# The assembly of a triangular inverse, moved from the scan's chain of steps into a background process

## The chip, the core and the metric

One core of a Trainium2 chip runs the whole kernel. The time is the device time of one execution in microseconds (us). The engines are PE (TensorE: matrix products, with its weight loads as PEld), DVE (VectorE), ACT (ScalarE), POOL (GpSimd) and SP (SyncE, which here only issues transfers). Each has its own queue of instructions and works through it in order; semaphores tie the queues together.

## The reference

One layer of a hybrid encoder on 2048 tokens of 1024 features, with 16 meta tokens ahead of them. One projection of `h` feeds two branches. Branch A is a gated DeltaNet with 8 heads: a short convolution, normed q and k, and a recurrence over chunks, in which a unit lower triangular system is solved for each chunk:

```python
lower = jnp.where(strict, jnp.einsum('bhnid,bhnjd->bhnij', k_beta, k) * decay, 0.0)
rhs = jnp.concatenate([v_beta, k_beta * jnp.exp(g_cum)[..., None]], axis=-1)
sol = lax.linalg.triangular_solve(lower + jnp.eye(CHUNK, dtype=f32), rhs, left_side=True, lower=True, unit_diagonal=True)
...
def step(S, inp):
    u_c, w_c, attn_c, q_c, k_c, gl_c = inp
    v_new = u_c - jnp.einsum('bhik,bhkv->bhiv', w_c, S)
    o_c = jnp.einsum('bhik,bhkv->bhiv', q_c, S) + jnp.einsum('bhij,bhjv->bhiv', attn_c, v_new)
    S = S * gl_c[..., None, None] + jnp.einsum('bhik,bhiv->bhkv', k_c, v_new)
    return S, o_c
```

Branch B is a sliding-window attention with sinks. Both branches are gated, projected, merged by gates computed from `h`, projected once more, added to `h` and layer-normed.

## The kernel before

**Tiles.** The 2048 tokens are worked in four blocks of 512 columns. A float32 operand is split into a high and a low part, and a projection of 128 output features over 512 tokens is 24 products of 128x128 by 128x512 (8 slices of the inner dimension, three products of parts each). These products, all on line L308, are the fill of the program: nearly all of PE's work.

**Order.** The program is one Python generator that writes instructions in the order in which every engine then takes them. `proj` yields behind every six products; this is one step, and one call of `tick()`. In `run(fill, streams, rates)` each step of the fill moves two streams by a fraction of a step: `chain`, which is `stage_c` of the groups 0 to 3 and then the attention `swa`, and `side`, which prepares the groups (`stage_b0`, `stage_b1`, `stage_b2`). Beside them run background processes, started with `bg(...)`: a process that yields a number n comes again n steps later, one that yields a condition comes when it holds. So the number of steps between two instructions sets how many of PE's products lie between them, and in every engine's queue what lies ahead of each.

**DeltaNet.** Two heads form a group, 128 tokens a chunk, four chunks a block. `conv_unit` writes the convolution of a projection: ACT copies the bank out, DVE adds three shifted products (L706, 128x512 each), ACT takes a tanh (L709), DVE multiplies (L711). `stage_b1(g)` transposes k (L779), forms the k·k products of the group in two banks, and DVE masks and scales them into `LT` (five small operations L796 to L800, then eight times L803), all eight 128x128 matrices of a group side by side. `stage_b2(g)` forms attn and transposes q (L876; ACT squares them, L878) and v.

`inverse(g)` is a background process that inverts the 32x32 diagonal blocks: a transfer to DRAM and back rearranges them, POOL solves them column by column (L829, L831), another transfer brings them back as `XT`, and after `DMA[5]` = 4 steps POOL copies XT into LT (L845).

`stage_c(g)` begins by putting the rest of the inverse together. DVE transposes XT into XN (L894, 128x256), ACT copies it into N64; PE forms `py` (L907, 16 small products), ACT copies it into Y (L912); PE forms `px` (L917 and L919, 24 products), ACT copies it into N64 and LT; then the same for 64x64 blocks with `py2`, Y2 and `px2`. Five plain yields of the chain lie between. Then comes the scan over the four chunks, in three parts a chunk: k·S (L958) into the bank `pks`, and R on DVE (L961); pw = LT·R (L966), q·S (L968), and wd from pw on DVE (L971) and ACT (L973); pu (L979) and the new S on DVE (L981). `out` is a background process that two steps later adds attn·wd (L947) in the same bank `pks` and DVE takes it up (L949).

**Banks.** Transposes, k·k, the scan and the assembly take their PSUM banks in turn from a pool of four, called `ps` in the trace; the projections have another four, `acc`. A bank is written again when the fourth request after it comes, and has to have been read by then.

**Other neighbours.** On DVE the low part of a split weight or of a branch output (L144, 128x1024) stands in the same queue, as do the small operations of the meta tokens in block 0 (`meta_heads`).

Of the kernel before, what the change touches and what calls it, by code (L numbers as in the profile page):

```python
# [73 lines left out]
def hybrid_kernel(  # L74
# [355 lines left out]
    def meta_heads(g, mstage, ok):  # L430

        h0 = 2 * g
        yield lambda: ok("kT", 1) and "es" in meta
        km, kt = yield from meta_conv(g, mstage, 0)
        pk = bank()
        for hh in range(2):
            T.matmul(pk[:NM, hh * NM:hh * NM + NM], km[:, hh, :], km[:, hh, :], start=True, stop=True)
# [155 lines left out]
    def block(b, nextx):  # L593
# [215 lines left out]
        def inverse(g):  # L809
# [36 lines left out]
            d["XT"] = XT  # L846

        def stage_b2(g):
# [4 lines left out]
            sq = tiny([P, 2, NC4], "sq")  # L853
# [32 lines left out]
        def stage_c(g):  # L886

            d, h0 = gr[g], 2 * g
            yield from until(lambda: "XT" in d and "vtok" in d)
            kT, qT, ktok, vtok, attn, LT = (d[n] for n in ("kT", "qT", "ktok", "vtok", "attn", "LT"))  # L890
            sq, cj, ce, XT = (d[n] for n in ("sq", "cj", "ce", "XT"))
            eg, neg = gates["eg"], gates["neg"]
            XN = tiny([P, 8, 32], "XN", 1)
# [1 line left out]
            N64 = tiny([64, 8, 64], "N64", 1)
            if first and g == 0:
                G.memset(N64[0:32, :, 32:64], 0.0)
                state["N64"] = N64
            N64 = state["N64"]
            A.activation(N64[0:32, :, 0:32], XN[0:32], AF.Copy)  # L900
            A.activation(N64[32:64, :, 32:64], XN[32:64], AF.Copy)
            yield

            py = bank()
            for m in range(8):
                for a, bq in ((0, 32), (64, 96)):
                    T.matmul(py[bq:bq + 32, m * 32:m * 32 + 32], LT[a:a + 32, m, bq:bq + 32], XN[a:a + 32, m, :],  # L907
                             start=True, stop=True, tile_position=(a, bq))
            Y = tiny([P, 8, 32], "Y", 1)
            for s in range(2):  # L910
                bq = 64 * s + 32
                A.activation(Y[bq:bq + 32], py[bq:bq + 32, 0:256].rearrange("p (m i) -> p m i", m=8), AF.Copy)  # L912
            yield
            px = bank()
            for m in range(8):
                for a, bq in ((0, 32), (64, 96)):
                    T.matmul(px[a:a + 32, m * 32:m * 32 + 32], Y[bq:bq + 32, m, :], XT[bq:bq + 32, m, :],  # L917
                             start=True, stop=True, tile_position=(bq, a))
                T.matmul(px[32:64, m * 32:m * 32 + 32], XT[32:64, m, :], Y[32:64, m, :], start=True, stop=True, tile_position=(32, 32))  # L919
            A.activation(N64[32:64, :, 0:32], px[32:64, 0:256].rearrange("p (m i) -> p m i", m=8), AF.Copy)  # L920
            for s in range(2):
                a, bq = 64 * s, 64 * s + 32
                A.activation(LT[a:a + 32, :, bq:bq + 32], px[a:a + 32, 0:256].rearrange("p (m i) -> p m i", m=8), AF.Copy)
            yield

            py2 = bank()
            for m in range(8):
                T.matmul(py2[64:128, m * 64:m * 64 + 64], LT[0:64, m, 64:128], N64[:, m, :], start=True, stop=True, tile_position=(0, 64))
            Y2 = s2([P, 8, 64])
            A.activation(Y2[64:128], py2[64:128, :].rearrange("p (m i) -> p m i", m=8), AF.Copy)  # L930
            yield
            px2 = bank()
            for m in range(8):
                T.matmul(px2[0:64, m * 64:m * 64 + 64], Y2[64:128, m, :], LT[64:128, m, 64:128], start=True, stop=True, tile_position=(64, 0))
            A.activation(LT[0:64, :, 64:128], px2[0:64, :].rearrange("p (m i) -> p m i", m=8), AF.Copy)
            yield
# [7 lines left out]
            def out(c, pks, wd):  # L944
                yield 2
                for hh in range(2):
                    T.matmul(pks[:, hh * P:hh * P + P], attn[:, hh, c, :], wd[:, 0, hh, :], start=True, stop=True)  # L947
                yield 2
                V.tensor_tensor(out=o[:, :, c, :], in0=pks[:, 0:256].rearrange("p (h d) -> p h d", h=2), in1=o[:, :, c, :], op=ALU.add)  # L949
                yield 1  # L950
                for hh in range(2):
                    A.activation(junk, o[:, hh, c, :], AF.Square, accum_out=so[:, hh, c:c + 1])
                d["so", c] = True

            for c in range(NC4):
# [558 lines left out]
```

## Time and profile before

| | |
|---|---|
| median of 3 runs (lowest, highest) | 2658.24 us (2656.61, 2660.33) |
| the profiled execution | 2659.29 us |
| its span, first to last instruction | 2657.5 us |
| PE busy, share of the span | 2606.1 us, 98% |
| DVE busy | 1573.0 us, 59% |
| ACT busy | 1223.3 us, 46% |
| POOL busy | 764.3 us, 29% |
| mean granted clock of PE, share of full | 0.992 |

Busy times are the sums of an engine's instructions; matrix products overlap and their ends are modelled. An engine can be idle as long as PE does not wait for it. The granted clock is given for any stretch; 1.00 is 2.4 GHz and 0.50 is 1.2 GHz. The four blocks end at about 721, 1361, 2002 and 2645 us.

### The profile page before, as it was taken

What the parts mean: (1) busy time and instruction counts of PE and PEld (TensorE: products, weight loads), DVE (VectorE), ACT (ScalarE), POOL (GpSimd) and SP (SyncE); (2) the same over time, 40 slices, a digit from 0 to 9 for tenths busy, and PEclk for the clock granted to TensorE, in tenths of its full rate; (3) what the DMA queues carried; (4) which work ended last, traced back from release to release, by engine and by line L of the source; (5) the groups of instructions that cost most, each with busy time, mean ns of one, the idle gap of its engine ahead of it and who ended that gap; (6) DMA issues with size and microseconds to landing.
All of it is one profiled execution on the core that took longest, in us unless ns stands there. A gap on an engine that the chain in (4) does not pass through costs nothing.

```text
span 2657.5 us, 44100 instructions
## 1 busy us (share of the span) xinstructions
PE 2606.1 (98%) x15308; PEld 2185.0 (82%) x15308; DVE 1573.0 (59%) x3959; ACT 1223.3 (46%) x3248; POOL 764.3 (29%) x1702
## 2 busy tenths in 40 slices
PE   9999999999999999999999999999999999999998
PEld 7777778888888888888887888888888788888886
DVE  6779858844464655762465564675347466476335
ACT  4556546542244544653324554565232455465422
POOL 2544324432055430110106433110102644111022
PEclk9999999999999999999999999999999999999999
DMA  7654556643574454664466445575347544466533
GB/s 256 202 177 166 190 185 186 203 159 102 192 251 148 144 173 143 206 196 149 150 213 194 136 148 168 168 212 180 122 158 237 176 143 149 153 202 207 167 101 136
DMA packets 243534, 461.63 MB, mean 174 GB/s; under 512 B 78024, under 2 KB 136160, under 8 KB 243312
## 3 DMA queue, kind: packets, MB, share of 16 engines
q1 hardware_dynamic: 243312, 458.82, 54.7%
q8 instruction: 121, 1.98, 0.3%
q14 instruction: 101, 0.83, 0.1%
HBM read 379.89 MB, written 78.82 MB: 173 GB/s over the span
## 4 chain that ended last, share of the span: by engine, by line
PE 61%; DVE 3%; POOL 2%; DMA 2%; ACT 1%; issue 1%; SPq 1%; DVEq 0%; POOLq 0%; ACTq 0%
PE acc L308 44%; PE ps L1127 2%; PE ps L1092 1%; POOL X L831 1%; POOL tm L829 1%; PE ps L968 1%; PE ps L958 1%; PE ps L966 1%; PE ps L979 1%; PE ps L947 1%; PE ps L1145 1%; DVE s L706 1%; PE acc L1395 1%; PE acc L1397 1%; PE acc L1398 1%; PE ps L858 1%
## 5 line engine op out<-in xcount | busy, mean ns | idle before, releaser
L308 PE MATMUL acc<-xh,wh 128*128 128x512 f32 x1800 | 740.3, 411 | 0.0
L308 PE MATMUL acc<-xl,wh 128*128 128x512 f32 x1800 | 711.2, 395 | 0.0
L308 PE MATMUL acc<-xh,wl 128*128 128x512 f32 x1800 | 476.3, 396 | 0.0
L308 PEld LDWEIGHTS acc<-xh,wh 128*128 128x128 f32 x1800 | 342.7, 190 | 60.7 <-issue 0.6
L308 PEld LDWEIGHTS acc<-xl,wh 128*128 128x128 f32 x1800 | 343.4, 191 | 58.7
L308 PEld LDWEIGHTS acc<-xh,wl 128*128 128x128 f32 x1800 | 331.2, 189 | 67.4 <-issue 0.5
L273 ACT ACTIVATE wh<-wr 128x1024 fp32r<-128x1024 f32 (+1 forms) x246 | 258.2, 1049 | 278.6 <-PE acc L308 158.8
L706 DVE SCALAR_TENSOR_TENSOR s<-st,cw,s 128x512 f32<-128x512 f32 x288 | 233.7, 812 | 70.3 <-ACT st L701 63.4
L144 DVE TENSOR_TENSOR wl<-wr,wh 128x1024 fp32r<-128x1024 f32 (+2 forms) x125 | 161.9, 1295 | 157.4 <-ACT wh L273 138.5
L308 PE MATMUL acc<-y,wh 128*128 128x512 f32 x1024 | 250.0, 392 | 0.0
L829 POOL TENSOR_TENSOR tm<-X,g 128x60 f32<-128x60 f32 (+24 forms) x496 | 169.8, 342 | 261.7 <-DMA g<-d 226.3
L308 PEld LDWEIGHTS acc<-y,wh 128*128 128x128 f32 x1024 | 189.1, 188 | 37.3
L308 PE MATMUL acc<-xh,wr 128*128 128x512 f32 x624 | 208.9, 402 | 0.0
L1244 POOL TENSOR_TENSOR g<-g 128x512 f32<-128x512 f32 x32 | 69.9, 2184 | 432.7 <-DVE g L1237 432.7
L831 POOL TENSOR_TENSOR X<-X,tm 128x60 f32<-128x60 f32 (+24 forms) x496 | 165.9, 335 | 38.9
L1237 DVE SCALAR_TENSOR_TENSOR g<-g,acc 128x512 f32<-128x512 f32 x64 | 44.0, 687 | 203.2 <-PE acc L308 203.0
L1073 POOL TENSOR_TENSOR g<-mo,slp 128x32 f32<-128x32 f32 x128 | 41.1, 331 | 389.3 <-DVE mn L1094 363.7
L1129 ACT ACTIVATE s<-ps 104x512 fp32r<-104x512 f32 (+2 forms) x128 | 76.5, 597 | 146.5 <-PE ps L1127 145.3
L308 PEld LDWEIGHTS acc<-xh,wr 128*128 128x128 f32 x624 | 116.2, 188 | 22.9
L1228 ACT ACTIVATE g<-acc,bg__162 128x512 f32<-128x512 f32 x64 | 44.2, 690 | 190.3 <-PE acc L308 189.7
L308 PE MATMUL acc<-y,wl 128*128 128x512 f32 x512 | 129.2, 390 | 0.0
L308 PE MATMUL acc<-xl,wr 128*128 128x512 f32 x312 | 122.2, 392 | 0.0
(329 smaller groups left out, 4668.4 us busy)
## 6 DMA issues: line engine op xcount, KB each, us to landing
wr<-in_wfm_dram SPq DMA_DIRECT2D x214, 512.0 KB
wl<-ws SPq DMA_DIRECT2D x165, 512.0 KB
wr<-ws SPq DMA_DIRECT2D x78, 512.0 KB
wh<-ws SPq DMA_DIRECT2D x75, 512.0 KB
ws<-wl SPq DMA_DIRECT2D x68, 512.0 KB
g<-kd SPq DMA_DIRECT2D x240, 96.0 KB
ws<-wh SPq DMA_DIRECT2D x38, 512.0 KB
wr<-in_wo_dram SPq DMA_DIRECT2D x32, 512.0 KB
```

What stands on the lines that cost most here:

```text
L144: eng.tensor_tensor(out=out_, in0=src, in1=f(hi), op=ALU.subtract)
L273: A.activation(hi[:, k], raw[:, k], AF.Copy)
L308: T.matmul(ps, w_[:, k, :], r_(k), start=(n == 0), stop=(n == 3 * NK - 1))
L706: V.scalar_tensor_tensor(out=acc, in0=st[:, 3 - d:TB + 3 - d], scalar=cw[:, s, 3 - d:4 - d], in1=acc, op0=ALU.mult, op1=ALU.add)
L829: G.tensor_tensor(out=tm[:, :n, :r], in0=X[:, :n, j:j + 1].to_broadcast([P, n, r]), in1=L[:, j:j + 1, j + 1:].to_broadcast([P, n, r]), op= ...
L831: G.tensor_tensor(out=X[:, :n, j + 1:], in0=X[:, :n, j + 1:], in1=tm[:, :n, :r], op=ALU.add)
L1073: G.tensor_tensor(out=sr[kv]["bias"][:, ch, :, 192:208], in0=mo[:, ch:ch + 1, :].to_broadcast([P, 2, NM]), in1=slp[:, 2 * kv:2 * kv + 2].u ...
L1127: T.transpose(out=pT[0:kt, j * 256 + rt * P:j * 256 + rt * P + P], in_=Pt[:, ch, rt, s + j * kt:s + j * kt + kt], identity=ident)
L1129: A.activation(ph[0:kt], pT[0:kt], AF.Copy)
L1228: A.activation(gt_[u][:, br, :], ps, AF.Tanh, scale=0.5, bias=bg_[:, 8 * br + u:8 * br + u + 1])
L1237: V.scalar_tensor_tensor(out=t[:, br, :], in0=t[:, br, :], scalar=1.0, in1=ps, op0=ALU.add, op1=ALU.mult)
L1244: G.tensor_tensor(out=m[:, u % 2, :], in0=t[:, 0, :], in1=t[:, 1, :], op=ALU.add)
```

## The change

The block from XN to `px2` leaves `stage_c` and becomes the end of `inverse(g)`, a background process. Its parts no longer lie one yield of the chain apart, but a number of steps, `JOIN`. The copy of XT into LT comes seven steps after its load instead of four. `stage_c` waits for `d["T"]`, the whole inverse, before it begins, and then starts with the scan. `out` requests a bank of its own instead of writing into `pks`. `cj`, `ce` and `sq` get three buffers. `meta_heads(g)`, which runs in block 0 alone, also waits until the meta tokens of group g - 1 are done, and its k·k products move down by one step. No instruction is added or removed on any engine.

```diff
-DMA = (1, 3, 4, 1, 2, 4)
+DMA = (1, 3, 4, 1, 2, 7)
+JOIN = (5, 4, 3, 3, 3)
...
     def meta_heads(g, mstage, ok):
-        yield lambda: ok("kT", 1) and "es" in meta
+        yield lambda: ok("kT", 1) and "es" in meta and (g == 0 or ("S", g - 1) in meta)
         km, kt = yield from meta_conv(g, mstage, 0)
-        pk = bank()
-        for hh in range(2):
-            T.matmul(pk[:NM, hh * NM:hh * NM + NM], km[:, hh, :], km[:, hh, :], start=True, stop=True)
...
+        pk = bank()
+        for hh in range(2):
+            T.matmul(pk[:NM, hh * NM:hh * NM + NM], km[:, hh, :], km[:, hh, :], start=True, stop=True)
+        yield 1
...
-            cj = tiny([P, 2, NC4], "cj")
+            cj = tiny([P, 2, NC4], "cj", 3)
...
         def inverse(g):
...
             yield DMA[5]
             for q in range(4):
                 G.tensor_copy(LT[32 * q:32 * q + 32, :, 32 * q:32 * q + 32], XT[32 * q:32 * q + 32])
-            d["XT"] = XT
+            d["XT"] = True
+            XN = tiny([P, 8, 32], "XN", 1)
+            V.transpose(out=XN.rearrange("p s i -> p (s i)"), in_=XT.rearrange("p s i -> p (s i)"))
...
+            A.activation(N64[0:32, :, 0:32], XN[0:32], AF.Copy)
+            A.activation(N64[32:64, :, 32:64], XN[32:64], AF.Copy)
+            yield JOIN[0]
+
+            py = bank()
...
+            yield JOIN[1]
+            px = bank()
...
+            yield JOIN[2]
+
+            py2 = bank()
...
+            yield JOIN[3]
+            px2 = bank()
...
+            yield JOIN[4]
+            d["T"] = True
...
         def stage_c(g):
-            yield from until(lambda: "XT" in d and "vtok" in d)
+            yield from until(lambda: "T" in d and "vtok" in d)
-            XN = tiny([P, 8, 32], "XN", 1)
...
-            d["T"] = True
-            def out(c, pks, wd):
+            def out(c, wd):
                 yield 2
+                pks = bank()
                 for hh in range(2):
                     T.matmul(pks[:, hh * P:hh * P + P], attn[:, hh, c, :], wd[:, 0, hh, :], start=True, stop=True)
...
-                bg(out(c, pks, wd))
+                bg(out(c, wd))
```

What this does to the queues shows in three places of DVE's, all in block 1; blocks 2 and 3 have the same. In the names, `XN` is the transposed XT, `sk`, `cj` and `ce` are the scales of a group, `g` are buffers of the large pool, `s` of the small one and `S` is the state of a group. The changed kernel's lines are shifted: L706 became L709, L711 became L714, L796 to L803 became L799 to L806, L894 became L851, L961 became L965, L971 became L975, L981 became L985, and L144 became L146.

The first place is the transpose XN of group 0. The kernel before, DVE:

```order
L711 SCALAR_TENSOR_TENSOR g_8931<-s_8909,s_8870 128x512
L894 STREAM_TRANSPOSE XN_8949<-XT_8874 128x256
L796 TENSOR_SCALAR sk_8728<-sk_8728 128x8
L797 RECIPROCAL cj_8912<-sk_8728 128x8
L798 TENSOR_TENSOR cj_8912<-cj_8912,gm4be_8122 128x8
L799 TENSOR_SCALAR ncj_8913<-cj_8912 128x8
L800 TENSOR_TENSOR ce_8914<-cj_8912,eg_8256 128x8
L803 SCALAR_TENSOR_TENSOR g_8911<-ps_8915,ncj_8913,g_8581 128x128 x4
L803 SCALAR_TENSOR_TENSOR g_8911<-ps_8916,ncj_8913,g_8581 128x128 x4
L706 SCALAR_TENSOR_TENSOR s_8941<-st_8939,cw,s_8941 128x512 x3
```

The changed kernel, DVE, the same place:

```order
L803 TENSOR_TENSOR ce_8930<-cj_8928,eg_8272 128x8
L806 SCALAR_TENSOR_TENSOR g_8927<-ps_8931,ncj_8929,g_8597 128x128 x4
L806 SCALAR_TENSOR_TENSOR g_8927<-ps_8932,ncj_8929,g_8597 128x128 x4
L709 SCALAR_TENSOR_TENSOR s_8957<-st_8955,cw,s_8957 128x512 x3
L851 STREAM_TRANSPOSE XN_9016<-XT_8890 128x256
L714 SCALAR_TENSOR_TENSOR g_8947<-s_8999,s_8957 128x512
```

The transpose has moved from ahead of the masks of group 1 to behind them and behind three convolution steps.

The second place is chunk 2 of the scan of group 0. The kernel before, DVE, from R of that chunk on:

```order
L961 SCALAR_TENSOR_TENSOR s_9566<-ps_9563,neg_8280,g_8673 128x128 x2
L971 TENSOR_SCALAR s_9586<-ps_9581,ce_8406 128x128 x2
L949 TENSOR_TENSOR g_8673<-ps_9464,g_8673 128x2x128
L706 SCALAR_TENSOR_TENSOR s_9577<-st_9575,cw,s_9577 128x512 x3
L981 SCALAR_TENSOR_TENSOR S_85<-S_85,eg_8256,ps_9632 128x128 x2
```

The changed kernel, DVE, from R of that chunk on:

```order
L965 SCALAR_TENSOR_TENSOR s_9634<-ps_9631,neg_8296,g_8689 128x128 x2
L799 TENSOR_SCALAR sk_9367<-sk_9367 128x8
L800 RECIPROCAL cj_9595<-sk_9367 128x8
L801 TENSOR_TENSOR cj_9595<-cj_9595,gm4be_8138 128x8
L802 TENSOR_SCALAR ncj_9596<-cj_9595 128x8
L803 TENSOR_TENSOR ce_9597<-cj_9595,eg_8272 128x8
L806 SCALAR_TENSOR_TENSOR g_9594<-ps_9598,ncj_9596,g_9141 128x128 x4
L806 SCALAR_TENSOR_TENSOR g_9594<-ps_9599,ncj_9596,g_9141 128x128 x4
L851 STREAM_TRANSPOSE XN_9665<-XT_9507 128x256
L709 SCALAR_TENSOR_TENSOR s_9624<-st_9622,cw,s_9624 128x512 x3
L975 TENSOR_SCALAR s_9683<-ps_9678,ce_8422 128x128 x2
```

Between R and wd of this chunk there now stand a group's scales and masks, a transpose and three convolution steps, where there was nothing; `ps_9678` (pw) is the bank that `ps_9598` was.

The third place is the scan of group 1 beside the second half of kT of group 3. The kernel before, DVE:

```order
L961 SCALAR_TENSOR_TENSOR s_10288<-ps_10285,neg_8280,g_9306 128x128 x2
L706 SCALAR_TENSOR_TENSOR s_10274<-st_10272,cw,s_10274 128x512 x3
L949 TENSOR_TENSOR g_9306<-ps_10171,g_9306 128x2x128
L971 TENSOR_SCALAR s_10334<-ps_10329,ce_8914 128x128 x2
L711 SCALAR_TENSOR_TENSOR g_10262<-s_10327,s_10274 128x512
```

The changed kernel, DVE, the same place:

```order
L985 SCALAR_TENSOR_TENSOR S_86<-S_86,eg_8272,ps_10240 128x128 x2
L709 SCALAR_TENSOR_TENSOR s_10231<-st_10229,cw,s_10231 128x512 x3
L965 SCALAR_TENSOR_TENSOR s_10288<-ps_10285,neg_8296,g_9277 128x128 x2
L146 TENSOR_TENSOR y_10297<-g_9317,y_10193 128x1024
L714 SCALAR_TENSOR_TENSOR g_10219<-s_10283,s_10231 128x512
```

The last operation of the convolution of kT now stands behind R and the low part of a branch output, where it stood behind wd.

## Rows read from the trace of the kernel before

**Rows 1.** Busy time by stretches: us, each engine, clock, DMA share, GB/s

```profile
721.00:1361.00 640.00, 637.38 (x3689) 539.21 (x3688) 356.96 (x892) 291.93 (x777) 165.70 (x412) 1.00 0.56 172
600.00:700.00 100.00, 100.00 (x443) 82.81 (x442) 38.49 (x37) 30.02 (x31) 17.51 (x8) 1.00 0.44 142
```

**Rows 2.** PE's waits, blocks 1 to 3: line, releaser: us, times, longest

```profile
PE ps L917 <- ACT Y L912: 6.7, 4, 3.7
PE ps L917 <- DMA d<-g: 2.3, 1, 2.3
PE ps L907 <- DVE sk L796: 1.2, 1, 1.2
```

**Rows 3.** Timelines, group 0's assembly: start, us, engine, operation [wait <- releaser]

```profile
811.66 0.45 DVE L894 STREAM_TRANSPOSE XN<-XT 128x256 f32<-128x256 f32 x1 [3.48 <-DMA XT<-d]
815.49 2.79 DVE L706 SCALAR_TENSOR_TENSOR s<-st,cw,s 128x512 f32<-128x512 f32 x3
818.31 0.63 ACT L709 ACTIVATE s<-s 128x512 f32<-128x512 f32 x1 [5.18 <-DVE s L706]
819.39 0.24 PE L917 MATMUL ps<-XT,Y 32*32 32x32 f32 x2 [2.25 <-DMA d<-g]
...
2095.29 0.45 DVE L894 STREAM_TRANSPOSE XN<-XT 128x256 f32<-128x256 f32 x1 [6.00 <-DMA XT<-d]
```

**Rows 4.** Busy time and clock in short stretches, columns as in rows 1

```profile
245.60:252.00 6.40, 3.67 (x23) 2.72 (x25) 5.71 (x27) 2.06 (x8) 5.22 (x18) 1.00 0.00 1
360.10:366.70 6.60, 6.05 (x18) 3.65 (x17) 5.11 (x16) 2.03 (x4) 2.37 (x1) 0.50 0.37 110
820.90:824.10 3.20, 3.20 (x9) 2.43 (x8) 2.25 (x3) 2.09 (x7) 0.00 (x0) 0.50 0.84 204
1459.20:1465.80 6.60, 6.12 (x59) 4.91 (x60) 2.92 (x4) 3.94 (x10) 1.91 (x8) 0.50 0.79 235
2096.00:2103.00 7.00, 3.51 (x44) 2.63 (x41) 6.11 (x16) 1.44 (x4) 6.35 (x9) 1.00 0.81 283
```

**Rows 5.** PE's timeline, parts of the scan and transposes of kT

```profile
867.86 0.61 PE L958 MATMUL ps<-S,g 128*128 128x128 f32 x4
869.69 0.60 PE L966 MATMUL ps<-s,g 128*128 128x128 f32 x4
...
934.41 0.60 PE L779 MATMUL ps<-cm,g 128*128 128x128 f32 x4
...
977.72 0.60 PE L966 MATMUL ps<-s,g 128*128 128x128 f32 x4
981.35 0.60 PE L979 MATMUL ps<-s,g 128*128 128x128 f32 x4
```

**Rows 6.** DVE's timeline at the same places, and a low part in block 0

```profile
174.56 1.21 DVE L144 TENSOR_TENSOR wl<-wr,wh 128x1024 fp32r<-128x1024 f32 x1
...
868.51 0.61 DVE L961 SCALAR_TENSOR_TENSOR s<-ps,neg,g 128x128 f32<-128x128 f32 x2 [0.24 <-PE ps L958]
...
876.76 0.13 DVE L796 TENSOR_SCALAR sk<-sk 128x8 f32<-128x8 f32 x1
877.68 2.16 DVE L803 SCALAR_TENSOR_TENSOR g<-ps,ncj,g 128x128 f32<-128x128 f32 x8
880.25 2.33 DVE L706 SCALAR_TENSOR_TENSOR s<-st,cw,s 128x512 f32<-128x512 f32 x3 [0.41 <-ACT st L701]
...
933.30 0.90 DVE L711 SCALAR_TENSOR_TENSOR g<-s,s 128x512 f32<-128x512 f32 x1
```

**Rows 7.** PE's waits in block 0, 104 to 721 us, columns as in rows 2

```profile
PE ps L779 <- DVE g L711: 5.5, 2, 3.0
PE ps L876 <- ACT g L878: 5.4, 2, 2.7
...
PE ps L979 <- DVE s L971: 1.7, 1, 1.7
PE ps L917 <- ACT Y L912: 1.3, 2, 1.2
```

More of the change, by code (lines that the diff above doesn't have):

```diff
@@ L845, in inverse @@
                 G.tensor_copy(LT[32 * q:32 * q + 32, :, 32 * q:32 * q + 32], XT[32 * q:32 * q + 32])
-            d["XT"] = XT
+            d["XT"] = True
+            XN = tiny([P, 8, 32], "XN", 1)
+            V.transpose(out=XN.rearrange("p s i -> p (s i)"), in_=XT.rearrange("p s i -> p (s i)"))
+            N64 = tiny([64, 8, 64], "N64", 1)
+            if first and g == 0:
+                G.memset(N64[0:32, :, 32:64], 0.0)
+                state["N64"] = N64
+            N64 = state["N64"]
@@ new lines, in inverse @@
+            A.activation(N64[0:32, :, 0:32], XN[0:32], AF.Copy)
+            A.activation(N64[32:64, :, 32:64], XN[32:64], AF.Copy)
+            yield JOIN[0]
+            py = bank()
+            for m in range(8):
+                for a, bq in ((0, 32), (64, 96)):
+                    T.matmul(py[bq:bq + 32, m * 32:m * 32 + 32], LT[a:a + 32, m, bq:bq + 32], XN[a:a + 32, m, :],
+                             start=True, stop=True, tile_position=(a, bq))
+            Y = tiny([P, 8, 32], "Y", 1)
@@ new lines, in inverse @@
+            for s in range(2):
+                bq = 64 * s + 32
+                A.activation(Y[bq:bq + 32], py[bq:bq + 32, 0:256].rearrange("p (m i) -> p m i", m=8), AF.Copy)
+            yield JOIN[1]
+            px = bank()
+            for m in range(8):
+                for a, bq in ((0, 32), (64, 96)):
+                    T.matmul(px[a:a + 32, m * 32:m * 32 + 32], Y[bq:bq + 32, m, :], XT[bq:bq + 32, m, :],
+                             start=True, stop=True, tile_position=(bq, a))
+                T.matmul(px[32:64, m * 32:m * 32 + 32], XT[32:64, m, :], Y[32:64, m, :], start=True, stop=True, tile_position=(32, 32))
@@ new lines, in inverse @@
+            A.activation(N64[32:64, :, 0:32], px[32:64, 0:256].rearrange("p (m i) -> p m i", m=8), AF.Copy)
+            for s in range(2):
+                a, bq = 64 * s, 64 * s + 32
+                A.activation(LT[a:a + 32, :, bq:bq + 32], px[a:a + 32, 0:256].rearrange("p (m i) -> p m i", m=8), AF.Copy)
+            yield JOIN[2]
+            py2 = bank()
+            for m in range(8):
+                T.matmul(py2[64:128, m * 64:m * 64 + 64], LT[0:64, m, 64:128], N64[:, m, :], start=True, stop=True, tile_position=(0, 64))
@@ new lines, in inverse @@
+            Y2 = s2([P, 8, 64])
+            A.activation(Y2[64:128], py2[64:128, :].rearrange("p (m i) -> p m i", m=8), AF.Copy)
+            yield JOIN[3]
+            px2 = bank()
+            for m in range(8):
+                T.matmul(px2[0:64, m * 64:m * 64 + 64], Y2[64:128, m, :], LT[64:128, m, 64:128], start=True, stop=True, tile_position=(64, 0))
+            A.activation(LT[0:64, :, 64:128], px2[0:64, :].rearrange("p (m i) -> p m i", m=8), AF.Copy)
+            yield JOIN[4]
+            d["T"] = True
@@ L852, in stage_b2 @@
             kT, qT, E, sk = d["kT"], d["qT"], d.pop("E"), d["sk"]
[L853 removed]
+            sq = tiny([P, 2, NC4], "sq", 3)
             attn = g4([P, 2, NC4, P])
@@ L888, in stage_c @@
             d, h0 = gr[g], 2 * g
-            yield from until(lambda: "XT" in d and "vtok" in d)
+            yield from until(lambda: "T" in d and "vtok" in d)
             kT, qT, ktok, vtok, attn, LT = (d[n] for n in ("kT", "qT", "ktok", "vtok", "attn", "LT"))
-            sq, cj, ce, XT = (d[n] for n in ("sq", "cj", "ce", "XT"))
+            sq, cj, ce = (d[n] for n in ("sq", "cj", "ce"))
             eg, neg = gates["eg"], gates["neg"]
-            XN = tiny([P, 8, 32], "XN", 1)
-            V.transpose(out=XN.rearrange("p s i -> p (s i)"), in_=XT.rearrange("p s i -> p (s i)"))
@@ L895, in stage_c @@
[L895 to L936, printed above, removed]
             if first:
                 yield from until(lambda: ("S", g) in meta)
-            d["T"] = True
```

2 lines of the change are left out of this document (1 added, 1 removed).

## The prediction

> **What bounds the kernel now.** I read the busy time by stretches first. In block 1 the TensorE (PE) is busy 637.38 of 640 us while VectorE (DVE), ScalarE (ACT) and GpSimd (POOL) are busy 357, 292 and 166 us [rows 1]. So only what makes PE stand still, or run at a lower clock, can move the end. Undisturbed, PE starts a product every 0.226 us (443 in 100 us) [rows 1]. Next come PE's waits by line. In blocks 1 to 3 nearly all of them belong to one place, the second pair of small products that assembles the inverse (`px`, L917): 6.7 us behind the ACT copy into Y (L912), 2.3 behind a DMA, and 1.2 at the first pair (L907), 10.2 us in all [rows 2]. Group 0 of each block is the one that waits.
>
> The engine rows tell how. DVE arrives at the transpose of XT (L894) at once and stands there 3.48 us, because the transfer of XT has not landed; behind it in DVE's queue lie the masks L803 and three convolution steps L706, which end at 818.28; ACT's tanh L709 waits 5.18 us for those, the Y copy stands behind that tanh, and PE reaches L917 and waits 2.25 us [rows 3]. After this wait, and after those of blocks 2 and 3 (up to 3.7 us [rows 2]), the granted clock is at 0.50, the lower of its two levels (1.2 GHz): for 3.2 us in block 1, 6.6 in block 2 and again 3.2 in block 3, for which block 1's row stands [rows 4]. At half speed half of such a stretch is lost: 6.5 us of 13.0.
>
> **What the change removes.** XN is now transposed behind its transfer by seven steps instead of four (a step is six products, 6 x 0.226 = 1.36 us), and `px` stands nine steps (12.2 us) behind XN, where it stood four (5.4 us). On DVE the masks and the L706 now lie ahead of the transpose (first order piece), so they no longer wait for the transfer. The longest of DVE's waits at L894 was 6.00 us, in block 3 [rows 3]; three more steps, 4.1 us, leave 1.9 of it, and 12.2 us lie between it and L917. I take all of 10.2 + 6.5 = **16.7 us** in blocks 1 to 3 as gone. It is a gain only as far as nothing else is late there, which is the next part.
>
> **What costs nothing by count.** Every instruction of the assembly stays (one transpose, nine ACT copies, 56 small matmuls per group); the loads of XT on SP's queue, POOL's four copies L845 and the ACT copies only move. POOL is busy a quarter of block 1, so three more steps in front of its copies are covered; if they were late, the next group's solve would be, which starts seven steps later. The scan of group 0 starts at step 81 instead of 69 (counting the yields), the attention at 185 instead of 174, and its last output is put down at step 272 instead of 261. The products that take it up come after step 283, where both streams are drained; in block 0 it is 286 against 287. So one step (1.36 us) of cover is left in block 0; without it PE would wait for the attention's output, at most a few us once. Third buffers for cj, ce and sq remove a wait that no row shows: nothing.
>
> **What it adds.** The scan runs 10 to 12 steps later against work that has not moved, and meets other neighbours. Three such places in each of blocks 1 to 3 can be priced.
>
> *A, pw of chunk 2 of group 0 (L966).* `out` now takes a bank of its own, so the four banks turn faster, and pw gets the bank of the first half of group 1's k·k products, which the first four L803 must have read. In the second order piece these stand behind R (L961). From PE's start on L958: DVE begins R at +0.65 (867.86 to 868.51), R 0.61, the five small operations 0.92 (876.76 to 877.68), half of 2.16 for four L803, 1.08: 3.26 us. PE gets to L966 1.83 us after L958 (867.86 to 869.69) [rows 5, 6]. Wait 1.4.
>
> *B, pu of the same chunk (L979).* PE: 1.83 + 1.43 + 3.63 (977.72 to 981.35) = 6.89. DVE: 3.26 + 1.08 + 0.45 for L894 + 2.33 for three L706 + about 0.6 for the two products of wd = 7.7 [rows 3, 5, 6]. Wait 0.8.
>
> *D, the second half of kT of group 3 (L779).* Before, DVE's last convolution step L711 ran 933.30 to 934.20 and PE began at 934.41, with nothing to spare [rows 5, 6]. In the third order piece R and a weight's low part (L144, 1.21 us) now stand before it: 0.65 + 0.61 + 1.21 + 0.90 = 3.4, less the 1.83 in which PE gets there from L958, as in A. Wait 1.5.
>
> None of these meetings occurs in the trace of before. Below, each is bounded by nothing (DVE ahead by a few tenths, as at 934.41); above by its wait plus 0.46 us, what three L706 took more at 815.49 than at 880.25 [rows 3, 6]. A gain is excluded: PE does not wait there now. I take the worked values, since each is a sum of rows: 3.7 us a block, **11.1 us** in three, bounds 0 and 15.
>
> *Block 0* carries the meta tokens as well, and nearly every meeting there becomes another. Waits that go: L917 1.3, the first of two at L779 5.5 - 3.0 = 2.5, L876 5.4, L979 1.7, together 10.9 [rows 7], and half of the 6.6 us at clock 0.50 after 360 us [rows 4], 3.3: 14.2. New places of the same kind, where PE in the new order stands one or two steps behind a DVE or ACT operation with a queue ahead of it: L966 twice, L779 twice, the meta tokens' products (now behind a gate), L876, and the transposes of group 0's output. Seven, at the mean of the four waits L779, L876 and L979, (2.5 + 5.4 + 1.7)/4 = 2.4: 16.8. Net **+2.6**, bounds -7 (only three of them real) and +8 (all at 2.7, the longest at L876, and as much time at the lower clock as before).
>
> **The sum.** -16.7 + 11.1 + 2.6 = -3.0. Against the profiled execution, 2659.29 us (span 2657.5), it is 2656.3. That execution lay 1 us over the median, 2658.24; the same difference gives **2655.2**, 0.11% faster. About 0.2% (5.3 us) is what a measurement of this kernel can tell from no change.
>
> **Rivals.** *R1: the new meetings are free.* If DVE runs ahead by one step at A, B and D, the 16.7 us stay gained and block 0 comes out even: 2641.5. For it: the same kind of meeting at 934.41 cost nothing, and DVE is idle 44% of block 1. Against it: at each of the three, DVE's rows add up to more than PE's.
>
> *R2, on the other side: the waits take the clock with them.* The place is A and D in blocks 1 to 3. The waits of 2.25 us and more at L917 were followed by the lower clock; the 1.2 at L907, which ended at 2095.9 us, was not, nor was one of 2.7 at L876 in block 0, which ended at 248.6 [rows 2, 4, 7]. It decides if A and D reach about 2.3: then 0.9 + 0.8 more idle and one stretch of 3.2 us, 1.6 lost, per block: 3 x 3.3 = 9.9, so 2665.
>
> The Trainium skill, "TensorE: Matmul & The Clock Gate", section "What's actually happening", has it that "the default state is throttled, and activity releases the throttle"; by that rule each new pause of PE is a chance to fall back, which is R2's time. The rows bear it out at L917 and not after the 1.2 and the 2.7; A, B and D were worked out shorter than the shortest wait with which it holds, so R2 is not the forecast.
>
> *R3: the change does not do what it says.* The wait at L917 stays, since the transfer of XT is late by more than the added steps, or another operation holds up the Y copy: 2658.2 + 11.1 + 2.6 = 2672. Against it: 12.2 us of products between XN and `px` against an ACT wait of 5.18 [rows 3].
>
> **How the numbers follow.** Forecast 0.48; its own range is 2649 to 2661 (faster 0.17, same 0.29, slower 0.02). R1 0.24 (0.22, 0.02, 0). R2 0.21 (0, 0.06, 0.15). R3 0.07 (0, 0.01, 0.06). Faster 0.39, same 0.38, slower 0.23. The range reaches from R1 to R2's end, 2641 to 2667, and leaves out R3 and the tails of block 0's bounds.
>
> **What would show it.** Right: no PE wait at `px` of group 0 and clock 1.00 there; PE waits of 1 to 2 us at pw of chunk 2 of group 0 behind the masks, at pu behind wd, and at kT's transposes behind the last convolution step, once each per block; block 0 with as much PE idle as before. R1: no PE wait of 0.5 us in blocks 1 to 3. R2: windows at clock 0.50 right after the new waits. R3: `px` still behind the Y copy. What would make it wrong: a meeting that I did not find in blocks 1 to 3, or block 0, where seven places were priced by a mean.

## The result and the profile after

The changed kernel takes 2675.75 us (median of six, 2675.22 to 2678.50), the kernel before 2658.0 beside it: 1.0067 times as long, interval 1.0054 to 1.0080. The forecast was 2655.2, the range 2641 to 2667. The page and the span:

```profile
PE 2614.0 (98%) x15308; PEld 2184.0 (82%) x15308; DVE 1575.9 (59%) x3959; ACT 1221.6 (46%) x3248; POOL 763.8 (29%) x1702
core 0: 2675.4 us, clock 0.991
```

PE's starts give the blocks' lengths, from the first product of one to that of the next: 734.0, 641.3, 641.3 and 642.9 us, where the kernel before has 716.9, 639.8, 641.4 and 643.3. So block 0 lost 17.1 us and the other three 1.0 together. PE's waits by line in blocks 1 to 3 (line, releaser, us in all, times, longest), against [rows 2]:

```profile
PE ps L970 <- DVE g L806: 3.9, 3, 1.3
PE ps L782 <- DVE g L714: 3.8, 3, 1.3
PE ps L1014 <- DVE s L1138: 1.1, 3, 0.4
PE ps L924 <- DVE g L714: 0.9, 3, 0.3
```

The waits at `px` (L917, now L874 and L876) have gone, and so has the lower clock in these blocks. In their place stand A (pw, L970) and D (kT, L782), once in each block, and four small ones, of which two are shown. In block 0 nearly every row is another than in [rows 7]. (L876 there is the transposes of v, not of q as said above, and L878 the scaled copy out of their bank; L876 is L924 here.)

```profile
PE ps L782 <- DVE g L714: 7.4, 2, 4.0
PE ps L512 <- DVE s L508: 4.2, 1, 4.2
PE ps L1131 <- DVE g L1117: 3.8, 6, 1.5
PE ps L924 <- DVE g L714: 3.7, 1, 3.7
PE ps L970 <- DVE s L965: 3.0, 2, 2.0
PE ps L1014 <- DVE g L997: 2.5, 1, 2.5
PE ps L1149 <- DVE s L1138: 2.1, 2, 1.6
```

Short stretches of block 0 (us, busy time of PE, PEld, DVE, ACT, POOL, granted clock, DMA share, GB/s), as in [rows 4]; two more, at 113 and 297 us, are like the second:

```profile
191.50:198.20 6.70, 4.51 (x16) 3.96 (x16) 3.60 (x8) 1.96 (x9) 1.21 (x3) 0.50 0.40 157
239.40:242.60 3.20, 3.20 (x13) 2.76 (x12) 2.44 (x7) 0.89 (x5) 2.73 (x9) 0.50 0.00 0
321.30:331.40 10.10, 8.86 (x36) 7.24 (x37) 4.02 (x9) 3.27 (x7) 8.42 (x30) 0.50 0.54 174
389.60:396.30 6.70, 6.70 (x30) 5.15 (x30) 1.86 (x3) 1.23 (x3) 0.00 (x0) 0.50 0.32 100
457.90:461.10 3.20, 3.20 (x13) 2.82 (x13) 3.10 (x15) 2.13 (x3) 0.14 (x1) 0.50 0.20 82
```

**Where block 0's time is.** For each kernel I took three numbers of block 0: its length, the sum of all of PE's waits, and the time that the trace has at clock 0.50, of which half is lost. What is left lies between 677.2 and 680.9 us in all of them, so waits and clock make nearly the whole difference. Each row is one traced execution.

| kernel | scans of block 0 start at step | length | waits | at 0.50 | length - waits - half | blocks 1 to 3 |
|---|---|---|---|---|---|---|
| before | 69, 99, 135, 167 | 716.9 | 27.5 | 20.5 | 679.2 | 639.8, 641.4, 643.3 |
| after | 81, 113, 147, 187 | 734.0 | 36.8 | 37.5 | 678.5 | 641.3, 641.3, 642.9 |
| e1 | 81, 113, 147, 180 | 733.4 | 37.5 | 37.5 | 677.2 | 641.3, 641.2, 642.3 |
| e2 | 69, 107, 147, 187 | 723.9 | 32.8 | 20.5 | 680.9 | 639.7, 641.3, 643.2 |
| e3 | 73, 102, 139, 169 | 720.5 | 30.5 | 20.5 | 679.8 | 639.8, 641.4, 640.7 |
| e7 | 81, 109, 143, 170 | 723.2 | 33.2 | 23.9 | 678.1 | 639.9, 641.6, 641.8 |
| e9 | 69, 101, 135, 169 | 727.8 | 36.9 | 23.9 | 679.0 | 635.0, 634.9, 636.7 |
| e8 | as before | 715.7 | 28.7 | 13.7 | 680.2 | 635.0, 634.9, 635.9 |
| e18 | as after | 701.7 | 20.1 | 6.8 | 678.2 | 641.3, 641.1, 642.2 |

The 17.1 us between the first two rows are 9.3 of waits and 8.5 of clock, less 0.7.

### The profile page after: what moved, and what is told of

Same layout as the page of the kernel before. It is cut to its first block, busy times and chain, and to the rows that moved or that the text cites. A ratio compares the mean times of both kernels' runs of the same rounds, so it can differ in the third digit from the quotient of the medians.

```text
span 2675.4 us, 44094 instructions
## 1 busy us (share of the span) xinstructions
PE 2614.0 (98%) x15308; PEld 2184.0 (82%) x15308; DVE 1575.9 (59%) x3959; ACT 1221.6 (46%) x3248; POOL 763.8 (29%) x1702
## 4 chain that ended last, share of the span: by engine, by line
PE 82%; DVE 9%; ACT 3%; POOL 2%; issue 2%; DMA 2%; SPq 0%; DVEq 0%; ACTq 0%; POOLq 0%
PE acc L310 58%; PE ps L1131 2%; PE ps L1096 2%; PE ps L970 1%; PE ps L972 1%; PE ps L983 1%; PE ps L962 1%; ACT g L1108 1%; PE acc L1399 1%; PE acc L1402 1%; PE acc L1401 1%; DVE s L709 1%; PE ps L1149 1%; PE ps L951 1%; POOL tm L832 1%
## 5 line engine op out<-in xcount | busy, mean ns | idle before, releaser
L709 DVE SCALAR_TENSOR_TENSOR s<-st,cw,s 128x512 f32<-128x512 f32 x288 | 229.7, 798 | 94.9 <-ACT st L704 86.4
L146 DVE TENSOR_TENSOR wl<-wr,wh 128x1024 fp32r<-128x1024 f32 (+2 forms) x125 | 161.9, 1295 | 142.8 <-ACT wh L275 123.9
L751 POOL TENSOR_TENSOR g<-cm,gh 128x256 fp32r<-128x256 f32 x64 | 53.0, 858 | 251.9 <-DVE gh L663 251.5
```

Source lines behind the costliest of these rows:

```text
L146: eng.tensor_tensor(out=out_, in0=src, in1=f(hi), op=ALU.subtract)
L709: V.scalar_tensor_tensor(out=acc, in0=st[:, 3 - d:TB + 3 - d], scalar=cw[:, s, 3 - d:4 - d], in1=acc, op0=ALU.mult, op1=ALU.add)
L751: G.tensor_tensor(out=gt[:, hh, c:c + 2], in0=tri.unsqueeze(1).to_broadcast([P, 2, P]), in1=part[:, c:c + 2, h0 + hh:h0 + hh + 1].to_broad ...
```

## Experiments

All times below are medians; the ratio to the kernel before, run on the same chip, has its interval in brackets. Theory J: the loss is block 0's, because the scan stands elsewhere there.

**Which part of the change.** Three parts undone or made alone.

```diff
# e1: the changed kernel, meta_heads as before
-        yield lambda: ok("kT", 1) and "es" in meta and (g == 0 or ("S", g - 1) in meta)
+        yield lambda: ok("kT", 1) and "es" in meta
...
# e2: the kernel before, with only this change to meta_heads
# e4: the changed kernel, out in the old bank
-            def out(c, wd):
+            def out(c, pks, wd):
                 yield 2
-                pks = bank()
...
```

> The changed kernel with meta_heads as before: no gate on the group before, the meta tokens' k·k products at their old place. The traces put the whole loss of about 17 us into block 0, half of it as waits of PE, half as lower clock. Theory J (the scan's later place in block 0 makes the loss; the meta change is one part of it, the wait of 4.2 us at the meta tokens' product L512 and the 3.4 us at half clock behind it): about 6 us off, 2668 to 2672. Rival M (the meta change is the cause; its gate puts the groups' meta work in a row and pushes its DVE operations in front of the transposes): the loss goes, 2657 to 2661. If the meta change is no part at all: 2675.

> The kernel before with the change to meta_heads alone. Theory J: the meta work meets the scan where it stood before, so 2656 to 2664, with blocks 1 to 3 unchanged. Rival M: block 0 alone gets longer by 12 to 17 us, 2670 to 2675.

> The changed kernel with out writing into the bank of k·S again, as before. Theory J with place A as predicted (pw waits for the masks because it gets their bank): the wait of 1.3 us at pw goes in blocks 1 to 3, 1.4 to 1.7 us a block, and a part of the 3.0 us at pw in block 0 with the low clock behind it; 2667 to 2672. Rival (the bank plays no part, pw's bank is late for another reason or pu waits instead): 2674 to 2677.

e1: 2674.16 us, 1.0067 [1.0051, 1.0083]; e2: 2666.18, 1.0037 [1.0023, 1.0052]; e4: 2677.01, 1.0084 [1.0069, 1.0099]. Neither theory has both right. By the traces the meta change alone lengthens block 0 by 7.0 us, and taken out of the changed kernel it gives back 0.6. The parts do not add. In e1 the wait at L512 is gone and 7.2 us at pw stand there. e1 lies at the value given for no part at all. e4 hit its rival: the wait at pw in blocks 1 to 3 is still 1.28 us. In its program `out` holds the older bank for so long that the other requests turn in three banks, and pw again gets the bank of the first half of the k·k products. So A comes from the scan's place; the prediction put it down to `out`'s bank.

**The wait at `px`.** `ce` and `sq` get three buffers as well.

```diff
# e3: the kernel before
-DMA = (1, 3, 4, 1, 2, 4)
+DMA = (1, 3, 4, 1, 2, 7)
-            cj = tiny([P, 2, NC4], "cj")
+            cj = tiny([P, 2, NC4], "cj", 3)
...
```

> The kernel before with XT taken up seven steps after its load instead of four, and the three buffers for cj, ce and sq; the assembly stays in the chain. Theory J: XN then stands behind the masks and the convolution steps, the wait at px of group 0 and the lower clock behind it go in blocks 1 to 3, and the scan comes three steps later instead of twelve; 2640 to 2650. Rival (three steps later costs as much as twelve, or the four steps between XN and px are too few, so that the Y copy is still late): 2656 to 2668.

2661.45 us, 1.0023 [1.0013, 1.0032]: the rival's number, by the first of its two reasons. The second did not happen: the wait at `px` is down to 0.5 us in three blocks, with the lower clock nearly gone. The scan, four steps later, meets others, in blocks 1 to 3:

```profile
PE ps L1127 <- DVE mn L1094: 4.8, 3, 1.6
PE ps L1127 <- DVE g L1113: 2.4, 3, 0.8
PE ps L779 <- DVE g L711: 2.4, 3, 0.8
PE ps L917 <- ACT Y L912: 0.5, 3, 0.2
```

**Blocks apart, and the assembly in fewer steps.** e5 and e8 keep the order of the kernel before in block 0 and use the process from block 1 on: `assemble` is the part from XN to `px2`, called at the end of `inverse(g)` with JOIN's pauses, or in block 0 in `stage_c(g)` with the chain's yields; e8 shortens JOIN, so that XN stays three steps later (step 62) and the scan begins at 69 again. e6 and e9 shorten JOIN in all blocks, e9 with `meta_heads` as before. e10 and e11 are e5 with the scan four and eight steps later.

```diff
# e5: the changed kernel
+            if not first:
+                yield from assemble(g, XT, True)
...
+            if first:
+                yield from assemble(g, d["XT"], False)
# e8: e5 and
-JOIN = (5, 4, 3, 3, 3)
+JOIN = (2, 2, 1, 1, 1)
# e6: the changed kernel with this JOIN; e9: and meta_heads as before
# e10: e5 with JOIN = (3, 3, 2, 2, 1); e11: e5 with JOIN = (4, 4, 3, 2, 2)
```

> The changed kernel for blocks 1 to 3, the order of the kernel before for block 0 (assembly in the chain, XT taken up after four steps, meta_heads as before). Theory J (the whole loss is block 0's, since its scan stands elsewhere; in blocks 1 to 3 what px gave back was spent at the new meetings): 2656 to 2661, blocks 1 to 3 at 641 us each as in the changed kernel. Rival (block 0 loses because of buffers or banks that the change ties to block 1, or blocks 1 to 3 lose as soon as block 0 is shorter): 2668 or more.

> The changed kernel with JOIN = (2, 2, 1, 1, 1) instead of (5, 4, 3, 3, 3): the assembly is done in seven steps, so in blocks 1 to 3 the scan of group 0 starts at step 69 as in the kernel before, with XN still behind the masks; in block 0 the groups 1 to 3 wait for the meta tokens as in the run with the meta change alone. Theory J: blocks 1 to 3 lose the px wait and get none of the new meetings, 10 to 16 us off the kernel before; block 0 stays 7 us over it; 2646 to 2655. Rival (four steps between XN and px are too few, so the Y copy is late as before): blocks 1 to 3 as before, 2662 to 2668.

> Block 0 in the order of the kernel before, blocks 1 to 3 as a process with JOIN = (2, 2, 1, 1, 1): scan of group 0 at step 69, XN at 62. Theory J: the loss of block 0 is gone and so is the px wait: 2641 to 2650, faster than both kernels. Rival (px is still late): 2655 to 2660.

> The changed kernel with JOIN = (2, 2, 1, 1, 1) in all blocks and meta_heads as before: the assembly is a process in block 0 too, and the scans of block 0 start at steps 69, 101, 135 and 169, where the kernel before has 69, 99, 135 and 167. Theory J (only the scan's place counts): block 0 at 715 to 720 us, in all 2636 to 2644. Rival (in block 0 the assembly's new places cost by themselves, with the scan where it was): block 0 at 724 or more, 2648 or more.

> Block 0 in the order of the kernel before, blocks 1 to 3 as a process with JOIN = (3, 3, 2, 2, 1): the scan of group 0 starts at step 73, four later than before. Theory J, in the form that every shift has its own meetings: 1 to 5 us a block over the 635 us of the run without a shift, as in the run with the later copy alone, which had waits at kT's transposes and in the attention at this shift; 2642 to 2655. Rival (only a shift of about twelve meets anything; four is as free as none): 2637 to 2641.

> As the run with a shift of four, with JOIN = (4, 4, 3, 2, 2): the scan starts at step 77, eight later than before. Theory J, every shift has its own meetings: 2 to 6 us a block over 635; 2645 to 2658. Rival (eight is as free as none): 2637 to 2641.

e5: 2658.93 us, 1.0012 [1.0002, 1.0021]: with block 0 as before the loss is gone, and blocks 1 to 3 stay at 642.0, 641.2 and 643.3. e6: 2646.20, 0.9962 [0.9948, 0.9977]. **e8: 2638.83, 0.9935 [0.9920, 0.9950], faster than both kernels.** e10: 2649.56, 0.9965 [0.9951, 0.9979]; e11: 2654.59, 0.9981 [0.9972, 0.9990]. Four of the five lie in the range of theory J, e8 2 us under it. In blocks 1 to 3 a shift of 0, 4, 8 or 12 steps gives about 635, 639, 639 and 641 us a block: every shift that was run has meetings, and the scan's old place has none. e8's block 1 (columns as above); PE waits nowhere in it, nor in blocks 2 and 3:

```profile
720.00:1355.00 635.00, 635.00 (x3688) 538.02 (x3687) 356.12 (x892) 291.45 (x777) 166.41 (x412) 1.00 0.56 174
```

Its XN in block 1 on DVE's and `px` on PE's timeline (start, us, engine, operation, no wait in brackets):

```profile
810.98 2.36 DVE L708 SCALAR_TENSOR_TENSOR s<-st,cw,s 128x512 f32<-128x512 f32 x3 [0.31 <-ACT st L703]
813.26 0.43 DVE L816 STREAM_TRANSPOSE XN<-XT 128x256 f32<-128x256 f32 x1
...
820.84 0.22 PE L839 MATMUL ps<-XT,Y 32*32 32x32 f32 x2
```

`px` stands four steps behind XN, as before; what matters is that XN comes behind the masks and L706 (here L708), and then its transfer has landed. The nine steps of the change were not needed.

e9 hit its rival and speaks against J in block 0: 2651.68 us, 0.9981 [0.9967, 0.9994], with block 0 11 us longer. Two of its scans still start two steps later than in the kernel before, so it does not fully part the assembly's places from the scan's. e6, which has the meta change besides, has a block 0 of 720.8 us, 7.0 shorter than e9's: the change that costs 7.0 alone gains as much here.

**The scan later in block 0, nothing else.**

```diff
# e7: the kernel before (and three buffers for cj, ce, sq)
+            if first and g == 0:
+                for _ in range(6):
+                    yield
```

> The kernel before with six yields of the chain more ahead of the first scan of block 0 (and three buffers for cj, ce and sq): the scans of the four groups start at steps 81, 109, 143 and 170 instead of 69, 99, 135 and 167; the assembly stays in the chain, the meta change is not made. Theory J (the scan's place in block 0 makes the loss, whoever puts the inverse together): block 0 longer by 8 to 16 us, 2665 to 2673. Rival (it is the assembly as a process that costs, its transposes and copies at new places among the others): 2656 to 2661.

2664.71 us, 1.0033 [1.0020, 1.0046]; block 0 is 6.3 us longer, a little under the range. With e1, e2, e3, e6 and e9: the moves in block 0 that these runs made cost 4 to 17 us each.

**Is DVE too full there?** The edit names 16 low parts of block 0 (1.22 us each on DVE). By the instruction counts 15 of them leave DVE (3944 instructions instead of 3959); the sixteenth was POOL's already. They go first to POOL (e12 to e14), then to nobody (e15 to e17: a transfer of another weight fills the tile).

```diff
# e12 (changed kernel), e13 (before), e14 (e8)
+    pool.update(range(11, 43, 2))
     return r, pool
# e15 (changed kernel), e16 (before), e17 (e8)
+        if 11 <= i < 43 and i % 2 == 1:
+            SY.dma_start(out=f(lo), in_=saved[i - 8][0])
+            return
```

> The changed kernel with every other of the 32 low parts of block 0's weights 11 to 42 made by POOL instead of DVE (16 operations of 1.22 us leave DVE's queue; the trace has POOL at 2.38 us for one). Nothing is moved in the order. Theory Q (block 0 loses because DVE is nearly full there and everything that PE waits for stands in DVE's queue, wherever the scan is put): the waits and the lower clock of block 0 fall, 8 to 16 us, 2660 to 2668. Rival P (what counts is the exact order at a few places, and POOL's solve, which then comes later, gives new waits): 2672 to 2685.

> The kernel before with the same 16 low parts made by POOL. Theory Q: block 0 of this kernel has 19 us of waits behind DVE and ACT too, so it gains, but less than the changed kernel: 3 to 9 us, 2649 to 2655. Rival P: 2656 or more.

> Block 0 in the order of the kernel before, blocks 1 to 3 with JOIN = (2, 2, 1, 1, 1), and the same 16 low parts made by POOL. Theory Q: 3 to 9 us under the run without it, 2630 to 2636. Rival P: 2639 or more.

e12: 2690.67 us, 1.0123 [1.0107, 1.0138]; e13: 2676.85, 1.0077 [1.0060, 1.0093]; e14: 2658.59, 1.0004 [0.9992, 1.0016], 20 us over e8. All slower. The reason is in e13's rows:

```profile
241.46 2.39 POOL L145 TENSOR_TENSOR wl<-wr,wh 128x1024 fp32r<-128x1024 f32 x1
243.80 1.75 POOL L763 TENSOR_TENSOR g<-g,cm 128x512 f32<-128x512 f32 x1
...
241.65 2.75 DVE L712 SCALAR_TENSOR_TENSOR g<-s,s 128x512 f32<-128x512 f32 x1
244.32 0.59 DVE L982 SCALAR_TENSOR_TENSOR S<-S,eg,ps 128x128 f32<-128x128 f32 x2
244.84 1.80 DVE L145 TENSOR_TENSOR y<-g,y 128x1024 fp32r<-128x1024 f32 x1
```

The last convolution step (L712, L711 of before) reads two tiles in SBUF. It starts while POOL makes a low part and ends 0.55 us behind POOL's 243.85, 2.75 us instead of 0.68. L982, which reads a bank, ran beside POOL's next operation in its usual time. The eighteen of this line in 104 to 420 us took 1.18 us on average, before 0.73, and PE waits for them. The Trainium skill says so, "SBUF — State Buffer", section "Who interferes with whom": a DVE instruction with two inputs in SBUF contends with a GpSimd instruction that reads SBUF, and the one that comes second blocks. The trace agrees. So these runs did not test the load.

> The changed kernel without 16 of DVE's low-part operations in block 0 (weights 11, 13 to 41): the subtraction is left out, and the low part is filled by a transfer of another saved weight, so the output is not the layer's. No other engine gets work for it. It is the test of a full DVE that the runs with POOL could not be, since there DVE's operations with two inputs in SBUF stood still while POOL worked. Theory Q (block 0 loses because DVE is nearly full): 20 us less on DVE; block 0 from 734 to 714 to 722 us, in all 2656 to 2664. Rival P (the loss hangs on a few particular meetings, of which these operations are no part): 2670 to 2680.

> The kernel before without the same 16 operations (output not the layer's, as in the run beside it). Theory Q: block 0 gains too, but less: 717 to 705 to 713 us, in all 2646 to 2654, so that the gap between the two kernels shrinks from 17 to about 10 us. Rival P: 2652 to 2662.

> Block 0 in the order of the kernel before and blocks 1 to 3 with JOIN = (2, 2, 1, 1, 1), without the same 16 operations (output not the layer's). Theory Q: 4 to 12 us under the run with them, 2627 to 2635. Rival P: 2635 to 2643.

e15: 2674.95 us, 1.0062 [1.0046, 1.0079]; e16: 2660.53, 1.0010 [1.0000, 1.0021]; e17: 2642.39, 0.9942 [0.9926, 0.9957]. All three hit rival P. The added transfers are not quite free: PE waits once for one of them, 1.8 us in e16 and 1.2 in e17, and not at all in e15. In e15 DVE is busy 97.94 of 146 us from 104 to 250, where the changed kernel has 106.82, and the long waits are as they were (line numbers 3 up):

```profile
104.00:250.00 146.00, 134.29 (x1012) 107.67 (x1011) 97.94 (x268) 77.59 (x248) 68.46 (x170) 0.95 0.62 207
PE ps L785 <- DVE g L717: 6.5, 2, 4.2
PE ps L515 <- DVE s L511: 4.2, 1, 4.2
PE ps L927 <- DVE g L717: 4.0, 1, 4.0
```

So less load on DVE, by 15 operations, gains nothing. What stands right ahead does count. At the wait of 4.0 us in the changed kernel, with POOL beside it, and the same small operations for a later group at 292 us:

```profile
187.35 2.73 POOL L751 TENSOR_TENSOR g<-cm,gh 128x256 fp32r<-128x256 f32 x4
190.04 2.33 POOL L751 TENSOR_TENSOR g<-cm,gl 128x256 fp32r<-128x256 f32 x4
...
187.84 0.63 ACT L712 ACTIVATE s<-s 128x512 f32<-128x512 f32 x1 [0.42 <-DVE s L709]
...
188.25 0.20 DVE L485 TENSOR_TENSOR g<-g 2x55 f32<-2x55 f32 x1
188.48 0.51 DVE L487 TENSOR_TENSOR g<-g 2x55 f32<-2x55 f32 x1
...
192.77 0.17 DVE L487 TENSOR_TENSOR g<-g 2x15 f32<-2x15 f32 x1
192.87 0.67 DVE L714 SCALAR_TENSOR_TENSOR g<-s,s 128x512 f32<-128x512 f32 x1
...
193.69 1.09 PE L782 MATMUL ps<-cm,g 128*128 128x128 f32 x4 [4.01 <-DVE g L714]
...
292.38 0.20 DVE L485 TENSOR_TENSOR g<-g 2x55 f32<-2x55 f32 x1
...
294.39 0.17 DVE L487 TENSOR_TENSOR g<-g 2x15 f32<-2x15 f32 x1
```

Ten small operations of the meta tokens' solve (L485, L487), written in one step, hold DVE from 188.25 to 192.94 while the tanh has been done since 188.47. They take 4.69 us here and 2.18 at 292.38, where POOL has nothing to do. Both L485 and L487 read two tiles in SBUF, as L712 does in e13, and beside POOL's L751 one takes up to 0.54 us instead of 0.2. So by estimate (4.69 - 2.18) some 2.5 of the 4.0 us come from POOL. e2, the meta change alone, has the same ten at 196.47, 4.70 us long, ahead of a wait of 4.6. No run moved POOL's work away. At 238.9 us it is the norm of the scan's output (a dozen small operations and eight L997, 230.05 to 236.2) and three L709 ahead of the meta tokens' wc (L508); at 322.5 us the norm again. e18 leaves both kinds of burst out of block 0, the 30 operations of a group's meta solve and the norm:

```diff
# e18: the changed kernel
-            V.tensor_tensor(out=tm[:, :n, :r], in0=X[:, :n, j:j + 1].to_broadcast([2, n, r]),
-                            in1=L[:, j:j + 1, j + 1:].to_broadcast([2, n, r]), op=ALU.mult)
-            V.tensor_tensor(out=X[:, :n, j + 1:], in0=X[:, :n, j + 1:], in1=tm[:, :n, :r], op=ALU.add)
...
+                if not first:
                     rsqrt_small(ro, so, [P, 2, NC4], "rs")
-                for hh in range(2):
+                for hh in range(0 if first else 2):
```

> The changed kernel without two kinds of bursts of small DVE operations in block 0: the solve of the meta tokens (30 operations a group) and the norm of the scan's output (the Newton steps and eight scalings a group). They are left out, so the output is not the layer's; the order of the rest is not moved. In the trace of the changed kernel such a burst stands right ahead of the operation that PE waits for at three of the longest waits of block 0: 4.0 us at kT's transposes (193.7 us), 4.2 at the meta tokens' product (238.9) and 3.7 at v's transposes (322.5), and ahead of the 2.5 us at the transposes of the output. Theory R (these bursts, met at their new places, are the waits, and the lower clock follows them): the four waits go, 14 us, and up to 13 us of the lower clock's share; 2648 to 2662. Rival P2 (other operations are late by as much, and the waits stay or are taken over by the next in the queue): 2668 to 2677.

2648.73 us, 0.9968 [0.9958, 0.9978]: 27 us under the changed kernel. The busy times of e15 and of e18 (the changed kernel has 1575.9 on DVE), then e18's stretches and waits:

```profile
PE 2613.0 (98%) x15308; PEld 2183.0 (82%) x15308; DVE 1561.2 (58%) x3944; ACT 1223.3 (46%) x3248; POOL 752.8 (28%) x1701
...
PE 2598.1 (98%) x15308; PEld 2173.4 (82%) x15308; DVE 1531.8 (58%) x3763; ACT 1221.1 (46%) x3248; POOL 761.1 (29%) x1702
104.00:250.00 146.00, 141.30 (x1090) 113.05 (x1089) 97.16 (x242) 85.66 (x273) 73.12 (x173) 0.99 0.57 193
250.00:420.00 170.00, 168.96 (x1154) 140.43 (x1153) 101.47 (x254) 91.59 (x264) 53.37 (x98) 1.00 0.58 194
PE ps L1129 <- DVE g L1115: 3.6, 5, 1.5
PE ps L502 <- DVE s L498: 2.8, 1, 2.8
```

All four waits named in the expectation have gone, and of 37.5 us at the lower clock 6.8 are left. So the bursts make these four waits, 14.4 of the 36.8 us of the changed kernel's block 0. e18 takes more from DVE than e15, 44 us of busy time against 15, so the two are not the same dose; but what e15 took gave nothing, and the four waits stood in it. None of the four stands at its place in the kernel before (PE began the same transposes of kT at 198.6 and of v at 319.8 with 0.1 us of idle or none). How much of the 17 us between the two kernels the bursts explain was not run: the kernel before has the same bursts, and no run left them out there.

## Why the prediction was wrong

**The gain: right.** 10.2 us of waits and half of the time at 0.50 went from blocks 1 to 3: 17.0 us by the traces, 16.7 forecast.

**A, B and D: two of three right in size.** A: 1.4 us forecast, 1.28 measured. D: 1.5, 1.26. B: 0.8, and PE did not wait.

```profile
887.41 0.61 PE L962 MATMUL ps<-S,g 128*128 128x128 f32 x4
888.05 0.61 DVE L965 SCALAR_TENSOR_TENSOR s<-ps,neg,g 128x128 f32<-128x128 f32 x2 [3.11 <-PE ps L962]
...
889.50 2.16 DVE L806 SCALAR_TENSOR_TENSOR g<-ps,ncj,g 128x128 f32<-128x128 f32 x8
890.68 0.71 PE L970 MATMUL ps<-s,g 128*128 128x128 f32 x4 [1.28 <-DVE g L806]
894.13 0.60 DVE L975 TENSOR_SCALAR s<-ps,ce 128x128 f32<-128x128 f32 x2
894.53 0.75 PE L983 MATMUL ps<-s,g 128*128 128x128 f32 x4
...
943.38 1.21 DVE L146 TENSOR_TENSOR y<-g,y 128x1024 fp32r<-128x1024 f32 x1
944.51 0.88 DVE L714 SCALAR_TENSOR_TENSOR g<-s,s 128x512 f32<-128x512 f32 x1
945.45 0.66 PE L782 MATMUL ps<-cm,g 128*128 128x128 f32 x4 [1.26 <-DVE g L714]
```

At A, R, the scales and the masks run without a gap, as worked out. At B, PE came 7.12 us after L962 and DVE was done at 7.32, with 6.89 and 7.7 forecast. pw did wait for the masks in the bank named, but what the prediction gave as the reason, `out`'s new request, was wrong (e4).

**Blocks 1 to 3: 1.0 us longer, 5.6 shorter forecast.** The waits of after sum to 11.9 us, near the 11.1 forecast, but by luck: four small meetings that were not in it (o's and v's transposes, the attention) stand in place of B. This term was too small. Against e8, whose three blocks take 1905.8 us without any wait, the changed kernel's 1925.5 are 19.7 us longer, not 11.1; some 7 of them are in no wait row (1925.5 - 11.9 is 1913.6, and the kernel before, less its waits and half of its 13.6 us at 0.50, has 1906.9). In one place a late start cost more than the idle time in its row: from L962 to L970 PE took 3.27 us, 1.44 more than the 1.83 of [rows 5], where the row has 1.28. That accounts for a part; the rest was not settled.

**Block 0: 17.1 us, 2.6 forecast. This is the step that failed.** The waits were nearer: 9.3 us more, with 16.8 - 10.9 = 5.9 forecast. The clock was the larger miss: 3.3 us of gain forecast, 8.5 of loss measured, 11.8 of the 14.5 missed. The term gave new waits no price at the lower clock, and even its upper bound held "as much time at the lower clock as before". And no place was worked out: seven meetings were priced by a mean, though the order would have shown the bursts ahead of them, ten or twenty rows at some 0.2 us and more; that ten of them would take 4.7 us beside POOL it would not have shown. One reading in the term is off: the 2.5 us at L779 that go are the later of the two waits there (at 279.9 us); the first, 3.0, stays, as 3.4.

**The rivals.** R3's time, 2672, was nearest, but its mechanism did not happen. R2's mechanism did, in the other place: none of the new waits in blocks 1 to 3 drew the clock down, and in block 0 waits of 1.65 us (before the stretch at 457.9) and 1.97 (before 297) did, shorter than the 2.25 that the prediction took as the point. In the kernel before, one of 2.7 did not. The length of one wait does not decide it, and the order does not either: that wait stands, 2.6 to 2.7 us long, in e5, e8, e10 and e11 too, whose block 0 is one and the same program; e8's was not followed by clock 0.50, the others were, for 3.4 to 6.8 us. So the clock's share of one trace is partly chance. Still, the block 0 of before, e5, e8, e10 and e11 has 10.2 to 20.5 us at 0.50, and that of after and e4 37.5 and 44.4. What decides it was not tried. R1 is what e8 makes true: 2638.8, with 2641.5 forecast.

## What to carry to other kernels

A block that differs from the others (here the first, with the meta tokens) gets its own count of meetings, each read in the order: for every instruction that the busiest engine waits for, what stands ahead of its releaser in the queue, small operations in bursts above all, and what POOL does beside them. When a wait comes from one operation that stands too early, move that one by a few steps and keep the rest of the schedule where it was: e8, with the same process in shorter pauses and block 0 left as it was, gains 0.65% where the change lost 0.67%. Where PE is the bound, price each new wait with the lower clock that may follow.

## What was not expected of the hardware

Leaving out the same 15 operations of DVE changed the time by less than 4 us; giving them to POOL cost 15 to 20: DVE's operation with two SBUF inputs stood for up to 2.82 us instead of 0.69 while POOL worked. The changed kernel has the same effect without any edit: ten small operations took 4.69 us beside POOL's L751 and 2.18 without. The lower clock followed a wait of 1.65 us in one place and not one of 2.7 in another, and the same wait in one run and not in the next: the 1.65 us of the changed kernel stands in e6 and e18 too, and there the clock stays at 1.00.
